# One scale for fifteen weight tiles and one for v, found in the prologue of a hybrid attention block

## The chip, the cores and the metric

The kernel runs on one core of one Trainium2 chip. A core has five engines that run their own instruction streams side by side: TensorE (PE, with weight loads shown as PEld), VectorE (DVE), ScalarE (ACT), GpSimd (POOL), and SyncE (SP), which here issues nearly all DMA transfers. The metric is the time of one execution in device microseconds (us). Three runs of the kernel before took 502.83, 505.03 and 505.9 us; the median is 505.03.

## The reference

One encoder layer on 1024 tokens of width 1024, in float32. One projection gives the queries, keys, values and gates of two head groups. Group A has 8 heads with a neighbourhood of 8 rows x 16 columns on a 16 x 64 token grid and a learned bias per head. Group B has 8 query heads on 2 key/value heads, rotary positions, a window of 128 tokens to each side and a sink logit.

```python
h = x @ w_in                                   # 1024 x 3328
q_a, k_a, v_a, z_a, q_b, k_b, v_b, z_b = split(h)   # 512 x4, 512, 128, 128, 512
y_a = neighborhood_attention(q_a, k_a, v_a, rel_pos_bias)
y_b = windowed_gqa_with_sink(rotary(q_b), rotary(k_b), v_b, sink)
mixed = concatenate([y_a * silu(z_a), y_b * silu(z_b)])
y = mixed @ w_out
out = layer_norm(2 ** 0.25 * x + y, ln_gain, ln_bias)
```

## The kernel before

**Numbers.** For accuracy near float32 a product is made of three passes over a high and a low part of each operand. For q, k and z the parts are float16: `x` is scaled by a power of two that suits its largest absolute value and split into `xf` (L477, L482). The weights of a *column tile* (128 of the columns of `w_in`, in two halves of 256 KB) are scaled by a power of two too. The power comes from the sum of the tile's absolute values: ScalarE sums each half with an Abs activation (`w_scan`, L183), one small matmul with a matrix of equal entries adds the 128 partitions (L196, "the total"), and a chain of some eight small VectorE instructions (L200 to L215) makes from it the scale `wsc`, its inverse `inv`, and what later steps need of it: `sg` for the scores, `rsg` for the bias, `vscb` for the gates. `w_split` then makes the float16 halves `wh` (ScalarE, L164) and `wl` (GpSimd, L169 and L170).

**The stages.** First the V projection in another format with three passes (L431, to 63.7 us); beside it `x` is loaded a second time and split. `v` has a scale per column group: VectorE keeps a running maximum `vmax` over all of v (L497, L498), five transposes bring it to where it can be reduced (`v_scale`, L566), five more spread the result (`v_spread`, L580), and `v_part` (L594) scales, casts and splits each of 8 row blocks and writes them to DRAM, from where `window` (L797) copies four windows for group A. At the same time the first 6 column tiles of 21 (NPRO = 6; `ORDER` gives zb0, z0, zb1, kb, qb0, z1) are projected. Each takes 48 matmuls of 128x512 (`project`, L332, the matmul is L356); the events of the V part are hung on the count of these 288 matmuls by `run_to`.

Then comes the attention in 128 units (64 of group B, then 64 of group A). A unit is: scores (L703, L704), a VectorE instruction that adds the bias and finds the maximum (L711), the exponential on ScalarE (L727), a split of the probabilities in two float16 parts (ScalarE L737, VectorE L738), a DMA transposition (L741), the products with v some units later (L766), and per four units the division by the sum (L775) and transposes (L786, "OT") in the bank "ot", whose result is multiplied by the gate. That bank is also the one into which the totals of L196 go. The remaining 15 column tiles and the first part of the output projection are fed between the units, about 6 matmuls per unit (`FILL_AT`, `pump_to`). The last stage is the output projection (L890) with the residual and the layer norm (`final`, L907).

**Order.** Within a `manual_schedule` region every engine gets its instructions as written. The kernel before has several such regions: the V part, the prologue tiles in two calls of `run_to`, and the attention with `final`; a planner may interleave instructions of different regions. What the column tiles need of ScalarE, VectorE, GpSimd and SP during the attention isn't written at its place but put in a queue per engine (`enq`). Per unit `pop` takes ND = 1 instruction (or a chain as one) from VectorE's queue, NA = 1 from ScalarE's and NP = 2 from GpSimd's, those with the lowest `prio` first; the chain of a scale has priority 0. `need` forces what must come before the next step. `rope` makes the rotary parts of q and k of group B (cast L286, shuffle L287, products L288 and L289, sum L290), and `split_q` and `split_k` the two parts of q and k (`hi` L234 and L236 on ScalarE, `lo` L240 and L242 on VectorE).

**Buffers.** `x` in its three-pass format fills 16 buffers of 4 KB per partition (`big`). The float16 `xf` takes 8 of them again when the V projection is through with them; the others stay empty until the output weights come. Weight halves go through four buffers `wr`: the load of half m + 4 (L153) is issued when `w_split` of half m is done.

Of the kernel before, what the change touches and what calls it, by code (L numbers as in the profile page):

```python
# [30 lines left out]
NPRO = 6  # L31
FILL = ORDER[NPRO:]
# [18 lines left out]
def hybrid_block(ctx, tc, xT, x, wt, wv, wo, bias, sink, gain, lbias, cos, sin, bmask, out):  # L51
# [4 lines left out]
    big = ctx.enter_context(tc.tile_pool(name="big", bufs=16))  # L56
# [13 lines left out]
    def pair_tile(name):  # L70
        return big.tile([128, 2, 512], F32R, tag="big", name=name)

    xh, xl, x16h, x16l = {}, {}, {}, {}
    for half in range(2):
        for k in range(KT):
            t = pair_tile(f"x{half}{k}")
            xh[half, k], xl[half, k] = t[:, 0, :], t[:, 1, :]
# [9 lines left out]
    vsc = const.tile([128, 6], F32, name="vsc")  # L87
    vscb = const.tile([128, 8], F32, name="vscb")
# [3 lines left out]
    wm = const.tile([128, 2 * NT], F32, name="wm")  # L92
    wg = const.tile([128, NT], F32, name="wg")
    wsc = const.tile([128, NT], F32, name="wsc")
    inv = const.tile([128, NT], F32, name="inv")
    sg = const.tile([128, 8], F32, name="sg")
    rsg = const.tile([128, 4], F32, name="rsg")
# [15 lines left out]
    ENG = ("act", "dve", "pool", "sp", "pe")  # L113
# [12 lines left out]
    def enq(eng, fn, *deps, prio=1):  # L126
        op = Op(eng, fn, deps, prio)
        if clock["step"] is None:
            op.emit()
        else:  # L130
            queues[eng].append(op)
        return op

# [22 lines left out]
    def w_split(m):  # L156
# [15 lines left out]
        scale = wsc[:, m // 2:m // 2 + 1]  # L172

        o = enq("act", hi, scale_ops[m // 2], prio=0.5)
# [4 lines left out]
    w_ops, stk_ops, load_ops, scale_ops, scan_ops = {}, {}, {}, {}, {}  # L179

    def w_scan(m):
        def scan():
            nc.scalar.activation(junk, raws[m].rearrange("p k c -> p (k c)"), AF.Abs, accum_out=wm[:, m:m + 1])  # L183

        if m < NH:
            scan_ops[m] = enq("act", scan, load_ops.get(("w", m)))

    def w_scale(n):
        if n >= NT:
            return  # L190
        name, cell = ORDER[n], {}
        kind, p = name.rstrip("0123"), int(name[-1]) if name[-1].isdigit() else 0

        def total():
            cell["ps"] = bank("ot")
            nc.tensor.matmul(cell["ps"][:, 0:2], ones, wm.bitcast(BF16)[:, 4 * n + 1:4 * n + 4:2], start=True, stop=True)  # L196

        def chain():
            g, ps, v = wg[:, n:n + 1], cell["ps"], inv[:, n:n + 1]
            nc.vector.tensor_reduce(g, ps[:, 0:2], axis=mybir.AxisListType.X, op=ALU.add)  # L200
            nc.vector.tensor_scalar_max(g, g, 2.0 ** -30)
            nc.vector.tensor_scalar(g.bitcast(I32), g.bitcast(I32), 0x7F800000, None, op0=ALU.bitwise_and)
            nc.vector.tensor_scalar(wsc[:, n:n + 1].bitcast(I32), g.bitcast(I32), 0x7F800000, None, op0=ALU.bitwise_xor)  # L203
            tanh = kind[0] == "z" and n > 2
            nc.vector.tensor_scalar(v, g, xrs, 0.25 if tanh else 0.5, op0=ALU.mult, op1=ALU.mult)
            if tanh:
                e, c = (4 + p, 4 + p // 2) if kind == "zb" else (p, p)
                nc.vector.tensor_mul(vscb[:, e:e + 1], vsc[:, c:c + 1], v)
            if kind[0] == "q":
                i = p if kind == "q" else 4 + p  # L210
                nk = ORDER.index("kb" if kind == "qb" else f"k{p}")
                nc.vector.tensor_scalar(sg[:, i:i + 1], v, inv[:, nk:nk + 1], -0.125 / QSCALE ** 2,
                                        op0=ALU.mult, op1=ALU.mult)
                if kind == "q":
                    nc.vector.reciprocal(rsg[:, p:p + 1], sg[:, p:p + 1])  # L215
# [167 lines left out]
    with ExitStack() as vctx:  # L383
# [119 lines left out]
        with tc.manual_schedule():  # L503
# [16 lines left out]
            for j in range(10):  # L520
                x2_load(j)
# [630 lines left out]
```

## Time and profile before

| | |
|---|---|
| median of 3 runs | 505.03 us |
| the profiled execution | 499.32 us, span 497.5 us |
| V projection | to 63.7 us |
| six prologue tiles | 63.7 to 138.3 us |
| attention and 15 tiles | 138.3 to 401.0 us |
| output projection | 401.0 to 489.5 us |
| last row's norm | 489.5 to 497.5 us |
| mean granted TensorE clock | 0.990 |

All durations below are of the profiled execution, which took 499.32 us by the same clock as the runs; its span is what the instructions cover. In the rows of groups stand the line, engine, operation, the tensors written and read, shapes and the count, then the busy time, the mean duration in ns, and the idle time of that engine just before, with what ended it. In the rows of waits stand the waiting instruction, what it waited for, and the total, the number of times and the longest in us. In timelines the first two numbers are start and length; matmuls overlap in the array, so a row of several can be longer than their distance.

### The profile page before, as it was taken

The page shows a single profiled execution, that of the slowest core. Times are in us where ns is not written, and L with a number is a line of the kernel's source. Part 1 is how long each engine was busy: PE and PEld are TensorE (multiplying, and loading weights), DVE is VectorE, ACT ScalarE, POOL GpSimd, SP SyncE. Part 2 cuts the span into 40 slices and gives each one's busy share as a digit, 9 for nine tenths or more (in the row PEclk, how much of TensorE's full clock was granted, in tenths as well). Part 3 has the DMA queues.
Part 4 walks back from the last instruction along what each step waited for, and adds up shares of the span by engine and source line. Part 5 has one row for each costly group of instructions (what it writes and reads, how often), then busy time and mean ns, then how long its engine had stood idle before and what let it go on. Part 6 is the DMA issues. An engine that isn't in the chain of part 4 may idle for free.

```text
span 497.5 us, 9558 instructions
## 1 busy us (share of the span) xinstructions
PE 457.3 (92%) x3262; PEld 296.1 (60%) x3262; DVE 371.6 (75%) x926; ACT 295.6 (59%) x701; POOL 225.5 (45%) x231
## 2 busy tenths in 40 slices
PE   8999999969899999798898898999999999999993
PEld 6999954423345455354455454556554677788883
DVE  5885979776657988887887877887777747559644
ACT  4639533544667887777778886877877737002101
POOL 0005943697437334854223745633674505314521
PEclk9999999998999999999899999999999999999998
DMA  7793141445546665576388999999986976535211
GB/s 254 260 293 129 60 143 43 127 127 170 190 90 142 108 136 109 114 121 116 90 170 205 204 208 197 235 215 207 224 176 157 208 166 232 174 145 190 107 42 63
DMA packets 134688, 78.95 MB, mean 159 GB/s; under 512 B 101360, under 2 KB 117744, under 8 KB 134384
## 3 DMA queue, kind: packets, MB, share of 16 engines
q1 hardware_dynamic: 134496, 78.20, 64.6%
q8 instruction: 25, 0.41, 0.4%
q14 instruction: 23, 0.19, 0.2%
q10 hardware_dynamic: 144, 0.15, 0.1%
HBM read 47.91 MB, written 9.96 MB: 116 GB/s over the span
## 4 chain that ended last, share of the span: by engine, by line
PE 31%; DVE 11%; ACT 4%; DMA 4%; issue 4%; SPq 1%; POOL 1%; ACTq 0%; DVEq 0%
PE ps_pj L356 12%; PE ps_s L890 4%; PE ps_pj L890 4%; PE ps_t L890 3%; PE ps_t L766 3%; DMA tr<-split 3%; DVE split L738 2%; DVE sn L711 2%; PE ps_ot L890 2%; PE ps_s L703 1%; PE ps_s L704 1%; DMA wor<-in_wo 1%; DVE m L824 1%; ACT split L737 1%; DVE qs L240 1%
## 5 line engine op out<-in xcount | busy, mean ns | idle before, releaser
L356 PE MATMUL ps_pj<-xf,wh 128*128 128x512 f16 x672 | 204.0, 382 | 5.5 <-DVE qs L240 3.3
L356 PE MATMUL ps_pj<-xf,wl 128*128 128x512 f16 x336 | 128.3, 382 | 0.0
L356 PEld LDWEIGHTS <-wh 128*128 128x128 f16 x672 | 62.6, 98 | 75.5 <-issue 9.2
L727 ACT ACTIVATE ps_s<-sn,nm 128x385 f32<-128x385 f32 (+3 forms) x128 | 70.4, 550 | 46.4 <-DVE nm L711 45.3
L738 DVE SCALAR_TENSOR_TENSOR split<-ps_s,split 128x384 f16<-128x384 f32 (+2 forms) x128 | 65.6, 512 | 28.1 <-ACT split L737 27.3
L169 POOL TENSOR_SCALAR wr<-wr,wsc 128x512 f32<-128x512 f32 x42 | 34.8, 827 | 98.4 <-ACT wh L164 93.9
L737 ACT ACTIVATE split<-ps_s 128x384 f16<-128x384 f32 (+2 forms) x128 | 57.4, 448 | 6.7 <-DMA tr<-split 4.9
L356 PEld LDWEIGHTS <-wl 128*128 128x128 f16 x336 | 33.0, 98 | 38.6 <-issue 1.1
L170 POOL TENSOR_TENSOR wl<-wr,wh 128x512 f16<-128x512 f32 x42 | 50.7, 1209 | 3.4
L703 PE MATMUL ps_s<-ks,qs 128*128 128x384 f16 (+2 forms) x128 | 39.8, 311 | 12.2 <-DVE split L738 7.6
L711 DVE CUSTOM_DVE_ANT_0 sn<-ps_s,bm,nsk 128x384 f32<-128x384 f32 (+1 forms) x64 | 40.8, 638 | 7.4 <-PE ps_s L704 6.8
L711 DVE CUSTOM_DVE_ANT_0 sn<-ps_s,bias,sg 128x288 f32<-128x288 f32 (+1 forms) x64 | 36.0, 563 | 12.7 <-PE ps_s L704 12.0
L704 PE MATMUL ps_s<-ks,qs 128*128 128x384 f16 (+2 forms) x128 | 39.7, 311 | 0.0
L766 PEld LDWEIGHTS <-tr 128*128 128x128 f16 (+1 forms) x1104 | 36.6, 98 | 2.0 <-issue 0.3
L164 ACT ACTIVATE wh<-wr,wsc 128x512 f16<-128x512 f32 x42 | 29.8, 711 | 12.4 <-DVE wsc L203 4.8
L678 POOL TENSOR_SCALAR bias<-bias,rsg 128x576 f32<-128x576 f32 (+1 forms) x24 | 19.2, 801 | 32.7 <-DMA bias<-in_bias 23.6
L945 ACT ACTIVATE sd<-mv,eps 128x1 f32<-128x1 f32 x8 | 2.4, 295 | 53.0 <-DVE mv L943 53.0
L890 PE MATMUL ps_s<-wo,m 128*128 128x512 f32 (+1 forms) x144 | 32.7, 375 | 0.3 <-DVE m L824 0.3
L270 POOL COPY ks<-ks 64x512 f16<-64x512 f16 x40 | 25.5, 644 | 9.9 <-ACT ks L234 3.7
L890 PE MATMUL ps_pj<-wo,m 128*128 128x512 f32 (+1 forms) x120 | 28.9, 378 | 0.7 <-DVE z L316 0.7
L890 PEld LDWEIGHTS ps_s<-wo,m 128*128 128x128 f32 x144 | 25.4, 188 | 5.6 <-DVE m L824 0.7
L704 PEld LDWEIGHTS <-qs 128*128 128x128 f16 x128 | 12.5, 98 | 26.6 <-issue 14.1
(154 smaller groups left out, 872.0 us busy)
## 6 DMA issues: line engine op xcount, KB each, us to landing
wr<-in_wt SPq DMA_DIRECT2D x42, 256.0 KB, 3.0
xraw<-in_xT SPq DMA_DIRECT2D x31, 256.0 KB, 3.5
bias<-in_bias SPq DMA_DIRECT2D x16, 288.0 KB, 3.4
wor<-in_wo SPq DMA_DIRECT2D x16, 256.0 KB, 5.7
xr<-in_x SPq DMA_DIRECT2D x8, 512.0 KB, 6.5
out<-xr SPq DMA_DIRECT2D x14, 256.0 KB, 2.0
bias<-in_bias SPq DMA_DIRECT2D x8, 384.0 KB, 3.9
wvraw<-in_wv SPq DMA_DIRECT2D x7, 320.0 KB, 4.5
```

The source lines that it names most:

```text
L164: nc.scalar.activation(h, raws[m], AF.Copy, scale=scale)
L169: nc.gpsimd.tensor_scalar(raw, raw, scale, 1.0, op0=ALU.mult, op1=ALU.mult)
L170: nc.gpsimd.tensor_sub(l, raw, h)
L356: nc.tensor.matmul(ps, a[:, k % 4, :], mv, start=(k == 0 and i == 0), stop=(k == KT - 1 and i == 2))
L703: nc.tensor.matmul(ps[:, :n], q, sl[0], start=True, stop=False)
L704: nc.tensor.matmul(ps[:, :n], q, sl[1], start=False, stop=True)
L711: nc.vector.tensor_tensor_reduce(sn[:, :n], ps[:, :n], bias_t, sg[:, c:c + 1], init, op0=ALU.add, op1=ALU.min, accum_out=nm)
L727: nc.scalar.activation(pt[:, :m], sn[:, :m], AF.Exp, bias=nm, scale=-1.0, accum_out=sm[:, k:k + 1])
L737: nc.scalar.activation(hl[:, :m, 0, :c], src, AF.Copy, scale=PSCALE)
L738: nc.vector.scalar_tensor_tensor(hl[:, :m, 1, :c], src, PSCALE, hl[:, :m, 0, :c], op0=ALU.mult, op1=ALU.subtract)
L766: nc.tensor.matmul(ps[:, HD * m:HD * m + HD], a, b_, start=(i == 0), stop=(i == len(mms) - 1))
L890: nc.tensor.matmul(ps, lh[:, ts], rh[:, cs], start=(e == EO[0] and i == 0), stop=(e == EO[-1] and i == 2))
```

## The change

The 15 column tiles of the attention get one common scale. In the prologue all 15 are loaded a first time, 512 KB each, into the buffers that `x` leaves free, 8 at a time (`sum_load`, at matmuls 1 to 8, and then each when a buffer is through). `sum_w` adds the absolute values of a whole tile in one instruction, at every 14th matmul from 28 on, on ScalarE (10 tiles) or VectorE (5). At matmul 237 `w_scale(NPRO)` makes one total of 15 columns and takes the largest, and one chain gives `wsc`, `inv`, `sg`, `rsg`, `vscb` and `invt` for all of them. With that, scans, totals and chains are no longer in the attention, TensorE's queue is dropped, and the tiles are still loaded by `w_load` for their split as before.

`v` gets one scale too. `v_max` reduces each row block of 640 columns in one VectorE instruction, `v_scale` (now at matmul 12, before at 66) needs one transposition and gives `vrs` and `vsc`. The multiplication of L605 is gone: the cast takes the scale. The copy `vb` goes from GpSimd to VectorE. `v_part` stands at matmuls 24 + 9t instead of 90 + 9t, and `window` at 124 + 12b instead of 178 + 14b.

The ordered region reaches from the V part to the end of the attention, and `final` stands behind it, outside. In the prologue the steps of `rope`, `split_q` and `split_k` are no longer emitted at once but at given numbers of matmuls later (`after`). ScalarE's queue counts as long from 5 waiting instructions instead of 3. The core of the diff:

```diff
-    big = ctx.enter_context(tc.tile_pool(name="big", bufs=16))
+    big = ctx.enter_context(tc.tile_pool(name="big", bufs=8))
+    def big_tile(name, shape=(128, 2, 512), dt=F32R):
+        n = taken[0]
+        taken[0] += 1
+        tag = "big" if n < 8 or 16 <= n < 24 or n >= 32 + NS else "big2"
+        return big.tile(list(shape), dt, tag=tag, name=name)
...
+    def enq(eng, fn, *deps, prio=1, after=0):
+        if clock["step"] is not None:
+            queues[eng].append(op)
+        elif after:
+            events.setdefault(ran[0] + after, []).append(op.emit)
+        else:
+            op.emit()
...
-        scale = wsc[:, m // 2:m // 2 + 1]
+        g = min(m // 2, NPRO)
+        scale = wsc[:, g:g + 1]
...
     def w_scale(n):
+        c, m = (2 * n, 2) if n < NPRO else (2 * NPRO, NS)
+        ps = bank("ot")
+        nc.tensor.matmul(ps[:, :m], ones, wm.bitcast(BF16)[:, 2 * c + 1:2 * (c + m):2], start=True, stop=True)
+        nc.vector.tensor_reduce(g, ps[:, :m], axis=mybir.AxisListType.X, op=ALU.add if n < NPRO else ALU.max)
...
+        if n == NPRO:
+            for i, (a, b) in enumerate(((nk, nq), (nk, NPRO), (NPRO, NPRO))):
+                nc.vector.tensor_scalar(sg[:, i:i + 1], inv[:, a:a + 1], inv[:, b:b + 1], -0.125 / QSCALE ** 2,
                                         op0=ALU.mult, op1=ALU.mult)
+            nc.vector.reciprocal(rsg, sg[:, 2:3])
-        o = enq("pe", total, scan_ops[2 * n], scan_ops[2 * n + 1])
-        scale_ops[n] = enq("dve", chain, o, prio=0)
...
-            o1 = enq("act", hi, dep, prio=prio)
-            ops.append(enq("dve", lo, o1, prio=prio))
+            o1 = enq("act", hi, dep, prio=prio, after=16 if dep else 0)
+            ops.append(enq("dve", lo, o1, prio=prio, after=20 if dep else 0))
...
+        def v_max(t):
+            nc.vector.tensor_reduce(vm[:, t:t + 1], v32[t], axis=AXX, op=ALU.max, apply_absolute_value=True)
...
         def v_scale():
+            nc.vector.tensor_reduce(vg, vm, axis=AXX, op=ALU.max)
+            ps = bank("s")
+            nc.tensor.transpose(ps[:, :128], vg.to_broadcast([128, 128]), identf)
+            nc.vector.tensor_reduce(vg, ps[:, :128], axis=AXX, op=ALU.max)
...
         def v_part(t):
-                nc.vector.tensor_sub(vt[:, :, 1, :], v3, vt[:, :, 0, :])
-                nc.gpsimd.tensor_scalar_mul(vb[:, t - 1], vt[:, 8:10], 1.0)
+                nc.vector.scalar_tensor_tensor(vt[:, :, 1, :], v3, vrs, vt[:, :, 0, :], op0=ALU.mult, op1=ALU.subtract)
+                nc.vector.tensor_copy(vb[:, t - 1], vt[:, 8:10])
...
-                nc.vector.tensor_mul(v32[t], v32[t], scr)
-                nc.scalar.copy(vt[:, :, 0, :], v3)
+                nc.scalar.activation(vt[:, :, 0, :], v3, AF.Copy, scale=vrs)
...
+        def sum_load(i):
+            if i < NS:
+                sums[i] = big_tile(f"ws{i}", (128, 2, 4, 128), F32)
+                nc.sync.dma_start(sums[i], wt[NPRO + i].rearrange("h p k c -> p h k c"))
+
+        def sum_w(i):
+            t, c = sums.pop(i).rearrange("p h k c -> p (h k c)"), 2 * NPRO + i
+            if i % 3 != 1:
+                nc.scalar.activation(t, t, AF.Abs, accum_out=wm[:, c:c + 1])
+            else:
+                nc.vector.tensor_reduce(wm[:, c:c + 1], t, axis=AXX, op=ALU.add, apply_absolute_value=True)
+            sum_load(i + 8)
+
+        at(12, v_scale)
+        for t in range(9):
+            at(24 + 9 * t, v_part, t)
+        for i in range(8):
+            at(1 + i, sum_load, i)
+        for i in range(NS):
+            at(28 + 14 * i, sum_w, i)
+        for b in range(4):
+            at(124 + 12 * b, window, b)
+        at(237, w_scale, NPRO)
...
-            pop("act", NA if i < M_AT[0] and len(queues["act"]) < 3 else 2)
+        pop("act", NA if i < M_AT[0] and len(queues["act"]) < 5 else 2)
...
+    ordered.close()
+    final()
```

406 lines of the change are left out of this document (175 added, 231 removed).

## The prediction

> **What bounds the kernel now.** I read the page's totals and its 40 slices first, then a table of busy time by stage, then the waits of TensorE in the longest stage, and last the order of single instructions around the largest waits.
>
> ```profile
> span 497.5 us, 9558 instructions
> PE 457.3 (92%) x3262; PEld 296.1 (60%) x3262; DVE 371.6 (75%) x926; ACT 295.6 (59%) x701; POOL 225.5 (45%) x231
> ...
> PEclk9999999998999999999899999999999999999998
> ```
>
> TensorE works 92% of the span, and no other engine over 75%. So the time is TensorE's work plus its gaps. The change adds no matmul of weight and takes only small ones away, so the question is which gaps go and which come. The table by stage (start:end, length, then busy time with instruction counts of PE, PEld, DVE, ACT, POOL, granted clock, DMA share, GB/s):
>
> ```profile
> 63.70:138.30 74.60, 65.39 (x304) 29.28 (x303) 55.53 (x117) 35.14 (x65) 42.90 (x42) 0.98 0.43 134
> 138.30:401.00 262.70, 242.21 (x2103) 135.34 (x2102) 207.78 (x619) 201.68 (x527) 130.01 (x143) 0.99 0.81 164
> 401.00:489.50 88.50, 87.54 (x468) 72.04 (x467) 55.14 (x102) 20.35 (x38) 29.94 (x22) 1.00 0.45 148
> 489.50:497.50 8.00, 0.00 (x0) 0.00 (x0) 4.18 (x9) 1.44 (x3) 1.68 (x2) 0.81 0.19 66
> ```
>
> The first row is the stage of the six prologue tiles, the second the attention with the other 15, the third the output projection with TensorE full, the fourth the last row's normalization. The attention has 262.70 - 242.21 = 20.5 us of idle TensorE. The waits there, TensorE's alone:
>
> ```profile
> PE ps_s L703 <- DVE split L738: 7.6, 9, 2.8
> PE ps_ot L786 <- DVE wg L200: 4.0, 4, 1.5
> PE ps_pj L356 <- DVE qs L240: 3.3, 3, 1.8
> PE ps_s L703 <- DVE sn L708: 2.2, 2, 1.9
> PE ps_pj L356 <- DVE ks L240: 2.2, 3, 1.0
> PE ps_pj L890 <- DVE z L316: 0.7, 1, 0.7
> ```
>
> They add to 20.0 us, nearly all of the idle time, and every one is for VectorE.
>
> **The attention, part by part.** Removed there are 26 scans on ScalarE, the 14 totals on TensorE, and 14 chains of small instructions on VectorE, one per later tile:
>
> ```profile
> L183 ACT ACTIVATE junk<-wr 128x512 bf16<-128x512 f32 x26 | 16.0, 616 | 0.0
> L183 ACT ACTIVATION_READ_ACCUMULATOR junk<-wr 128x1 f32 x26 | 4.9, 188 | 0.0
> L205 DVE TENSOR_SCALAR inv<-wg,xrs 128x1 f32<-128x1 f32 x14 | 2.8, 203 | 0.0
> ...
> L215 DVE RECIPROCAL rsg<-sg 128x1 f32<-128x1 f32 x4 | 0.7, 165 | 0.1
> ```
>
> ScalarE loses 16.0 + 4.9 = 20.9 us of its 201.7. The eight rows of VectorE's chain run from 2.8 us down to 0.7, some 14 us of its 207.8. Neither engine is full, so this work is worth nothing by itself. It counts where it stands ahead of something that TensorE waits for.
>
> (a) The OT transposes (L786) share their one bank with the totals, and wait for the chain to read it. Without totals this wait is gone: **4.0 us**. What is late next there is the divided output of L775, which the order has three units earlier, so I count nothing back.
>
> (b) The waits of L356 for the second parts of q and k (3.3 + 2.2) come from deferred instructions. VectorE takes one deferred instruction per unit (ND = 1), and the chain has priority 0. In the units where it takes the turn, the second `lo` of a q or k half slips one unit, and the next column tile's group finds its bank still in use. In the changed order that `lo` stands one unit earlier at those places (units 36, 60, 76, 84, 92 and 108 where before had the next one). Of 5.5 us I take **4.3**, since the casts ahead of the `lo` are now spread one per unit and can leave the short waits; the bounds are 2 and 5.5.
>
> (c) Two of the larger waits for other things, and what follows one of them (start, length, what, and in brackets the idle time before):
>
> ```profile
> 206.21 0.32 PE L703 MATMUL ps_s<-ks,qs 128*128 128x384 f16 x1 [1.95 <-DVE sn L708]
> ...
> 237.40 0.27 PE L703 MATMUL ps_s<-ks,qs 128*128 128x256 f16 x1 [2.81 <-DVE split L738]
> ...
> 238.61 1.04 PE L356 MATMUL ps_pj<-xf,wh 128*128 128x512 f16 x2
> 239.45 0.63 PE L356 MATMUL ps_pj<-xf,wl 128*128 128x512 f16 x1
> ```
>
> Both stand where a chain took VectorE's turn from the shuffle of the rotary part, so that the GpSimd products of it came late, ScalarE waited in order, and exp and split behind it came late too. In the changed order the shuffle stands at units 27 and 43 instead of 30 and 46. I take **2.0** for the first and **2.0** of 2.8 for the second, bounds 0 and 4.8. The other eight waits for L738, 4.8 us, are the length of exp, split and transposition of the unit itself; I leave them.
>
> (d) After the 2.81 us gap the matmuls start 0.42 us apart (238.61 to 239.45 for two), and the granted clock stays low for a while:
>
> ```profile
> 220.00:240.00 20.00, 17.19 (x169) 9.72 (x168) 13.80 (x42) 14.12 (x37) 10.58 (x11) 0.96 0.57 108
> 240.00:260.00 20.00, 18.86 (x150) 10.20 (x149) 17.60 (x50) 14.69 (x39) 5.61 (x6) 0.95 0.69 136
> ```
>
> That is 0.04 x 20 + 0.05 x 20 = **1.8 us**, back if the gap goes; else nothing. The Trainium skill speaks against taking it as the price of this gap: by "TensorE: Matmul & The Clock Gate", section "What's actually happening", the clock halves after a whole idle window of some 3.4 us, and 2.81 is less. By that rule this term would be nothing and the time 1.8 us higher. The trace has half speed right behind this gap, so I keep it.
>
> Attention: 4.0 + 4.3 + 2.0 + 2.0 + 1.8 = **14.1 us**.
>
> **The prologue, built anew.** Its six tiles are 288 matmuls. Where nothing interrupts them they take
>
> ```profile
> 340.26 1.29 PE ps_pj L356 x6
> ```
>
> 0.215 us each: 61.9 us at least, of the 74.6 measured. So 12.7 us are lost there before, the largest piece a total that waited 5.20 us for its scan behind the k casts, then ran at half speed:
>
> ```profile
> 112.87 0.16 PE L196 MATMUL ps_ot<-wm,ones 128*128 128x2 bf16 x1 [5.20 <-ACT junk L183]
> 112.90 1.01 PE L356 MATMUL ps_pj<-xf,wh 128*128 128x512 f16 x2
> ...
> 115.41 0.72 PE L356 MATMUL ps_pj<-xf,wh 128*128 128x512 f16 x2
> ```
>
> The six matmuls from 112.90 to 115.41 took 2.51 us instead of 1.29; with a few more, 1.4 us lost. In the changed order that scan stands at matmul 168 and the casts at 184, so this gap goes. The first attention unit's scores move from about matmul 238 to the end, so their wait for q goes too, as do the ten transposes of the v scale but one.
>
> What comes new is **v's single scale**. Its transposition stands on TensorE behind matmul 12, at 63.72 + 12 x 0.215 = 66.3. It waits for eight reductions on VectorE, and six of these stand behind the negation of the sink, which waits for a load:
>
> ```profile
> 64.43 0.43 SPq L537 DMA_DIRECT2D sk<-in_sink  x1
> ...
> 66.93 0.17 DVE L541 TENSOR_SCALAR nsk<-sk 128x8 f32<-128x8 f32 x1 [2.83 <-DMA sk<-in_sink]
> ...
> 36.37 0.17 DVE L530 TENSOR_REDUCE gm<-xm 128x1 f32<-128x16 f32 x1
> ...
> L440 DVE TENSOR_REDUCE xm<-x x16: 677/680/682, 20.2 to 35.7; 128x1 f32<-128x512 f32 x16
> ```
>
> A reduction of 512 elements took 0.68 us and one of 16 0.17, so one of 640 comes to about 0.81, my estimate. Six after 67.1 end at 72.0, and the small one of `vg` at 72.2: TensorE waits 72.2 - 66.3 = **5.8 us**, with all of tile 1 queued behind the transposition. By the gap at 112.87 another **1.4** goes at half speed (bounds for both: 4 and 8). One transposition takes 0.2.
>
> The sums of the 15 tiles lie beside the matmuls: ten Abs passes of 1024 on ScalarE (by L183's 0.616 + 0.188 for 512 about 1.2 us each) and five reductions on VectorE, one every 14 matmuls or 3.0 us. Between matmuls 24 and 96 ScalarE also has eight v casts,
>
> ```profile
> L606 ACT CAST vt<-v x8: 724/725/726, 86.0 to 105.5; 128x640 f16<-128x640 f32 x8
> ```
>
> and with scans, splits, outputs and three or four Abs passes I count 16.6 us of work in 15.5. I take **1.0** for that, bounds 0 and 3. The one total over 15 columns stands at matmul 237, 13 matmuls behind the last sum, 2.8 us for 1.2 us of work; I count nothing, and a wait there is in the 3.
>
> **The loads** are the unknown term. Fifteen of 512 KB, eight in one burst at about 68 us, pass through the one SP queue ahead of the weight loads that the prologue needs. Up to the load of half tile 9 I count 9.4 MB: 13 sums, three weight halves, cos and sin, six v parts. Its scan is needed at matmul 138: 63.7 + 5.8 + 1.4 + 138 x 0.215 = 100.6, less 0.8. So 9.4 MB have 31.6 us, or 0.297 MB/us. What the trace shows as rate:
>
> ```profile
> 280.00:300.00 20.00, 18.76 (x188) 11.11 (x189) 16.07 (x51) 15.40 (x43) 10.59 (x12) 1.00 1.04 207
> 20.00:40.00 20.00, 20.00 (x138) 20.00 (x138) 15.31 (x26) 10.01 (x23) 0.00 (x0) 1.00 0.83 263
> ...
> GB/s 0 0 0 0 0 0 0 0 0 0 0 0 246 322 291 299 174 56 229 393 328 361 415 382 377 388 328 131 33 0 0 0 0 0 0 0 0 0 0 0
> ```
>
> The first row is full engines with transpositions of many small packets among them (207); the second large rows at 0.83 of the engines' time, so 317 if full; the third the 15 us around 67, where cos, sin and weights alone were under way (40 slices of 0.375 us), with up to 415. A weight load took 3.0 us to land:
>
> ```profile
> wr<-in_wt SPq DMA_DIRECT2D x42, 256.0 KB, 3.0
> ```
>
> The sums have rows of 2 KB like the weights, but the v parts have short ones. At 0.263 everything is 4 us late, at 0.317 nothing. The nearest row is the second, at its full rate; I take **0.5**, bounds 0 and 4.4 (and 17, the rival below).
>
> Prologue after: 61.9 + 5.8 + 1.4 + 0.2 + 1.0 + 0.5 = 70.8, so **3.8 us** gained, with bounds of -3 and +8.
>
> **The end.** The final part is now outside the written order. The planner sets the gain's load earlier and three copies of output weights on VectorE ahead of the splits of m, and one matmul group stands ahead of the last OT transposes. The third stage has only 88.50 - 87.54 = 1.0 us idle, so there is nothing to win: I charge **1.4**, bounds 0 and 4.
>
> **Sum**: -14.1 - 3.8 + 1.4 = -16.5 us. The profiled execution took 499.32 us (497.5 of span and 1.8 around it), so its like would take 482.8. The median of the runs is 505.03, 5.7 above the profiled one; on that scale the time is **488.5**. The bounds of (b) to (d), of the prologue and of the end reach some 17 us to the slow side if all fall together and 14 to the fast one; a third of each is my range for this case alone, 483 to 494.
>
> **Rivals.** (1) *The loads decide; slower than before.* If the burst moves at the 207 GB/s of the full engines, the load of half tile 11 (12.4 MB behind 68.2) lands at 128.1 instead of the 110.9 at which its total stands: 17.2 us more of idle TensorE, and another 1.4 at half clock. Then 505.03 - 16.5 + 16.7 + 1.4 = 506.6. It decides when the rate falls under about 0.21 MB/us; above 0.3 it costs nothing. For it: one queue, and v's short packets in it. Against it: 263 at 0.83, and 415. The Trainium skill, "DMA: Bandwidth & Descriptors", section "Queues, rings and completion order", says that a queue's descriptors are taken in ring order on each DMA engine, so a weight load would not pass the sums; no row of before shows such a jam. (2) *The attention's waits are put off, not removed.* exp, split and transposition of a unit bound the rest, and what (b) to (d) give comes back as waits for L738. Then only 4.0 of 14.1 is kept: -4.0 - 3.8 + 1.4 = -6.4, 498.6. For it: L738 already leads the waits, and VectorE is 79% busy in that stage. Against it: most waits sit at the units where a chain stood. (3) *All waits go.* 20.0 + 1.8 in the attention, the prologue's +5.3 with neither load nor ScalarE waits, and no loss at the end: -27.1, 477.9.
>
> **Chances.** Forecast 0.57, (2) 0.20, (1) 0.13 with what lies between it and the forecast, (3) 0.07, and 0.03 for a time beyond all of these. One per cent, 5 us, is about what a measurement tells from no change. Faster by more than that (under 500): all of the forecast and (3), most of (2): 0.78. Slower (over 510): a third of (1) and the rest, 0.08; within 1% 0.14. The range goes from 480, half way from the forecast's low end to (3), to 504, into what lies between the forecast and (1); it leaves out most of (3) and of (1).
>
> **What the changed profile would show.** The waits of L786 for `wg` and most of those of L356 for L240 are absent; the attention stage is some 248 us; the clock rows are 0.99 or more. A gap of 5 to 6 us ends at the transposition of `vg` near 72, then matmuls start 0.42 us apart. No total (L196's successor) waits long for a scan; if one does, and the load before it took far more than 3 us to land, rival 1 is at work. The last stage stays within 2 us of 88.5. I am wrong if L738's waits grow past 12 us, if the prologue takes over 76 us, or if the last stage takes over 92.

## The result and the profile after

The changed kernel's median is 483.02 us (480.12 to 483.77, four runs), that of the kernel before 503.93 us with its fourth run (500.16 to 505.9). The ratio is 0.958, 95% interval 0.951 to 0.966: faster. Run again beside other kernels it gave 481.09 us and 0.959 (0.956 to 0.963). The prediction was 488.5 in a range of 480 to 504.

The page of the changed kernel: span and busy time of the engines, and the clock in 40 slices.

```profile
span 482.0 us, 9415 instructions
PE 452.4 (94%) x3239; PEld 294.5 (61%) x3239; DVE 349.4 (73%) x820; ACT 286.9 (60%) x661; POOL 216.1 (45%) x223
...
PEclk9999978999999999999998999999999999999997
```

Its time by stage, cut where the first prologue matmul, the 289th, the second unit's scores, the last unit's scores and the last matmul lie (columns as in the prediction):

```profile
61.56:135.85 74.29, 65.41 (x298) 29.20 (x297) 47.37 (x97) 42.96 (x78) 34.68 (x37) 0.93 0.72 243
137.14:385.28 248.14, 237.94 (x2076) 134.75 (x2075) 200.09 (x538) 185.78 (x477) 129.72 (x142) 0.99 0.93 174
385.28:474.00 88.72, 87.55 (x470) 72.39 (x469) 55.34 (x102) 20.07 (x38) 31.33 (x22) 1.00 0.43 141
474.00:482.00 8.00, 0.00 (x0) 0.00 (x0) 4.05 (x9) 1.44 (x3) 1.68 (x2) 0.63 0.18 66
```

Cut at the same instructions, the kernel before had 63.72 us to the first prologue matmul, 75.73 from there to the 289th, 261.60 of attention and 96.78 to the end:

| stage | before | after | difference | predicted |
|---|---|---|---|---|
| V projection | 63.72 | 61.56 | -2.2 | 0 |
| six tiles (1st to 289th matmul) | 75.73 | 74.29 | -1.4 | -3.8 |
| attention (2nd to last unit's scores) | 261.60 | 248.14 | -13.5 | -14.1 |
| from there to the end | 96.78 | 96.72 | -0.1 | +1.4 |
| span | 497.5 | 482.0 | -15.5 | -16.5 |

(The second unit's scores started 0.3 us before the 289th matmul in the one and 1.3 behind it in the other, which makes +1.6 in the sum. In the changed kernel six matmuls of the seventh tile stand ahead of these scores, in the kernel before none; so 1.3 of the attention's 13.5 us are work that only changed sides, and 12.2 are gained.) So the attention gave most of the gain. In the prologue one gap was exchanged for another.

The medians are 20.9 us apart, 5 more than the profiled executions. The profiled execution of the kernel before was the shortest of its first four at a granted clock of 0.990; its 36 runs beside the experiments (six slow ones left out) had 0.974 to 0.992, those of the changed kernel 0.98 to 0.99. Of the 36, the ten with a clock of 0.987 or more took 499.7 us on average, the nine under 0.980 took 504.1. So I read the rest of the difference as clock that the kernel before loses in most of its runs; the two go together in the runs, but no experiment changed the clock alone.

The waits of TensorE in the attention of the changed kernel (in us: total, times, longest):

```profile
PE ps_s L696 <- DVE split L731: 3.4, 8, 1.0
PE ps_s L696 <- DVE sn L701: 2.7, 2, 2.3
PE ps_t L759 <- DMA tr<-split: 2.3, 4, 1.6
PE ps_pj L881 <- DVE z L312: 0.7, 1, 0.7
PE ps_pj L348 <- POOL wl L183: 0.6, 1, 0.6
```

They were 20.0 us and are 9.7. Those of the OT transposes and of the q and k parts (4.0 and 5.5) are gone, those for the split (now L731) fell from 7.6 to 3.4, and 2.3 us of waits for the DMA transposition are new.

The timeline of TensorE and then that of VectorE in the changed kernel's prologue, at v's scale:

```profile
71.76 0.48 PE L550 MATMUL ps_s<-identf,vg 128*128 128x128 f32 x1 [7.44 <-DVE vg L548]
72.03 1.06 PE L348 MATMUL ps_pj<-xf,wh 128*128 128x512 f16 x2
72.88 0.63 PE L348 MATMUL ps_pj<-xf,wl 128*128 128x512 f16 x1
```

```profile
66.98 0.17 DVE L525 TENSOR_SCALAR nsk<-sk 128x8 f32<-128x8 f32 x1 [8.70 <-DMA sk<-in_sink]
67.06 4.45 DVE L483 TENSOR_REDUCE vm<-v 128x1 f32<-128x640 f32 x6
71.54 0.16 DVE L548 TENSOR_REDUCE vg<-vm 128x1 f32<-128x8 f32 x1
```

TensorE stood for 7.44 us behind a transposition that waited for six reductions, and these waited for the load of the sink, 4 KB that v's scale has no use for. Behind it two matmuls took 0.85 us, half speed. A second wait of the prologue is new too and stands in no term of the prediction: the 289th matmul waits for the gate `z`.

```profile
135.85 0.59 PE L348 MATMUL ps_pj<-xf,wh 128*128 128x512 f16 x2 [1.44 <-DVE z L312]
```

### The profile page after: what moved, and what is told of

The parts are those of the page before. It is cut to its first block, busy times and chain, and to the rows that moved or that the text cites. A ratio compares the mean times of both kernels' runs of the same rounds, so it can differ in the third digit from the quotient of the medians.

```text
span 482.0 us, 9415 instructions
## 1 busy us (share of the span) xinstructions
PE 452.4 (94%) x3239; PEld 294.5 (61%) x3239; DVE 349.4 (73%) x820; ACT 286.9 (60%) x661; POOL 216.1 (45%) x223
## 3 DMA queue, kind: packets, MB, share of 16 engines
q1 hardware_dynamic: 138576, 86.07, 74.3%
## 4 chain that ended last, share of the span: by engine, by line
PE 46%; DVE 16%; DMA 14%; ACT 8%; issue 8%; POOL 4%; SPq 3%; POOLq 0%; ACTq 0%; DVEq 0%
PE ps_pj L348 21%; PE ps_pj L881 5%; PE ps_s L881 5%; PE ps_t L759 4%; PE ps_t L881 3%; DMA tr<-split 3%; DMA wr<-in_wt 3%; PE ps_s L696 3%; PE ps_s L697 3%; DVE qs L237 3%; DMA xraw<-in_xT 2%; DVE split L731 2%; PE ps_ot L881 2%; DMA wvraw<-in_wv 2%; DVE sn L704 1%
## 5 line engine op out<-in xcount | busy, mean ns | idle before, releaser
L348 PEld LDWEIGHTS <-wh 128*128 128x128 f16 x672 | 64.2, 99 | 64.9 <-issue 4.3
L731 DVE SCALAR_TENSOR_TENSOR split<-ps_s,split 128x384 f16<-128x384 f32 (+2 forms) x128 | 65.6, 513 | 29.2 <-ACT split L730 28.2
L182 POOL TENSOR_SCALAR wr<-wr,wsc 128x512 f32<-128x512 f32 x42 | 30.6, 729 | 85.1 <-ACT wh L177 69.3
L265 POOL COPY ks<-ks 64x512 f16<-64x512 f16 x40 | 26.8, 675 | 10.8 <-ACT ks L229 7.0
L973 POOL TENSOR_TENSOR xr<-xr,gb 128x512 f32<-128x512 f32 x7 | 10.3, 1483 | 40.4 <-ACT xr L970 40.4
```

The source lines that it names most:

```text
L182: nc.gpsimd.tensor_scalar(raw, raw, scale, 1.0, op0=ALU.mult, op1=ALU.mult)
L348: nc.tensor.matmul(ps, a[:, k % 4, :], mv, start=(k == 0 and i == 0), stop=(k == KT - 1 and i == 2))
L731: nc.vector.scalar_tensor_tensor(hl[:, :m, 1, :c], src, PSCALE, hl[:, :m, 0, :c], op0=ALU.mult, op1=ALU.subtract)
```

## The experiments

The names of the kernels are those of their results. Unless said otherwise, "attention" is the stretch from the second unit's scores to the last unit's, and "prologue" that from the first prologue matmul to the 289th, both of the profiled execution. In the changed kernel they take 248.1 and 74.3, when run again 247.7 and 72.7. Some expectations name 136.5 and 75 us for the 289th matmul of the changed kernel, 64.7 for that of sink_late_nosums and 71.0 for that of sums_spread. These count two or three matmuls too far; the values are 135.85, 74.3, 64.05 and 70.55.

### The changed kernel again (after_again)

> The changed kernel once more, as the base for the kernels beside it. Every theory: 480 to 485, a ratio to the kernel before of 0.95 to 0.966, the wait for vg between 5 and 7.5 us.

481.09 us, ratio 0.959 (0.956 to 0.963). The wait for `vg` was 5.22 us in place of 7.44, since the sink landed 2.1 us earlier; the prologue is shorter by 1.6, as the half speed behind the gap lasted longer (13 steps of 0.427 us for 11). The gap thus varies by 2 us between executions.

### Scans alone, back in the attention (scans_back)

```diff
+    def scan_back(m):
+        if m < NH and clock["step"] is not None:
+            enq("act", lambda: nc.scalar.activation(junk, raws[m]..., AF.Abs, accum_out=wm2[:, m:m + 1]),
+                load_ops.get(("w", m)))
```

> Edit: in the changed kernel the 26 Abs scans of half tiles stand again in ScalarE's queue during the attention, their results unused; no totals, no chains. Theory A (what counted were the totals in the OT bank and the chains' turns on VectorE): the attention, from the second unit's scores to the last unit's, is 248 to 251 us as against 248.1 in the changed kernel and 261.6 before. Theory B (ScalarE's 20.9 us counted): 255 us or more.

477.81 us, ratio 0.946 (0.943 to 0.949). Its attention, by the same window:

```profile
135.25:380.04 244.79, 235.99 (x2076) 134.17 (x2075) 199.40 (x536) 199.47 (x529) 129.89 (x142) 1.00 0.91 177
```

ScalarE is busy 13.7 us longer than in the changed kernel (199.47 against 185.78), and the attention isn't longer: it is 3 us shorter, with no drop of the clock in it. The scans' work on ScalarE was worth nothing. That they make it shorter I don't claim; the ratio's interval lies apart from the changed kernel's in the other group of runs, and no run tells why.

### Totals and chains, back in the attention (chains_back)

```diff
+        for m in (2 * n, 2 * n + 1):          # scans of one element each
+            if m not in scan_ops:
+                scan_back(m)
+        o = enq("pe", total, scan_ops[2 * n], scan_ops[2 * n + 1])
+        scale_ops[n] = enq("dve", chain, o, prio=0)
-        o = enq("act", hi, load_ops.get(("w", m)), prio=0.5)
+        o = enq("act", hi, load_ops.get(("w", m)), scale_ops.get(m // 2), prio=0.5)
```

> Edit: in the changed kernel 13 totals into the OT bank and 13 chains of six small VectorE instructions with priority stand again in the attention, each behind two scans of one element on ScalarE; the results are unused. Theory A (totals and chains counted): the waits of the OT transposes come back with about 4 us, those of the q and k second parts with 3 to 5, the attention takes 255 to 262 us. Theory B (the scans' time counted): 248 to 251 us. If only the 4 us of the OT transposes come back, the attention takes about 252.

500.84 us, ratio 0.991 (0.988 to 0.994): the gain is gone but for one per cent. The attention and TensorE's waits in it:

```profile
134.64:399.34 264.70, 239.54 (x2089) 133.78 (x2088) 208.32 (x614) 190.00 (x529) 128.66 (x142) 0.99 0.82 164
```

```profile
PE ps_s L731 <- DVE split L766: 6.3, 7, 1.7
PE ps_s L731 <- DVE sn L736: 4.2, 3, 1.9
PE ps_pj L383 <- POOL wl L186: 3.6, 3, 1.5
PE ps_ot L814 <- DVE ch L219: 2.9, 4, 0.9
PE ps_pj L383 <- ACT wh L180: 2.6, 2, 2.0
PE ps_pj L383 <- ACT ks L264: 1.8, 1, 1.8
PE ps_pj L383 <- DVE qs L270: 1.7, 2, 0.9
PE ps_pj L383 <- DVE ks L270: 0.9, 1, 0.9
```

13 small matmuls, 26 reads of one element and 13 chains cost 16.6 us of attention (264.7 - 248.1), a little past the 255 to 262 expected. 2.9 us of it is the OT bank (the 4.0 of before) and 1.7 + 0.9 the q and k parts. The waits for the weights' parts `wl` and `wh` (3.6 + 2.6) weren't there before, though there too a tile was split only behind its chain; why they appear here isn't shown. So 16.6 us is what totals and chains cost in this order, and not the 12.2 that were gained.

### The kernel before without totals (no_total)

```diff
-            nc.vector.tensor_reduce(g, ps[:, 0:2], axis=mybir.AxisListType.X, op=ALU.add)
+            src = cell["ps"][:, 0:2] if "ps" in cell else wm[:, 2 * n:2 * n + 2]
+            nc.vector.tensor_reduce(g, src, axis=mybir.AxisListType.X, op=ALU.add)
...
+            scale_ops[n] = enq("dve", chain, scan_ops[2 * n], scan_ops[2 * n + 1], prio=0)
```

> Edit: the kernel before without the totals on TensorE during the attention: each chain reads the scans' sums of its own partition instead of the sum over all 128 partitions, so that step of the scale is left out. Scans and chains stay, and a chain still takes VectorE's one turn; chains and the rotary shuffles come some units earlier, since they no longer wait for a total's place. Theory A (the total's place and its bank make the price): the attention takes 247 to 253 us instead of 261.6. Theory B (scans' and chains' work on their engines make it): 258 or more.

493.79 us, ratio 0.979 (0.971 to 0.987).

```profile
139.15:392.74 253.59, 239.94 (x2084) 134.17 (x2082) 209.01 (x618) 199.95 (x527) 129.99 (x142) 1.00 0.84 169
```

The attention is 253.6 us, 8.0 less than before and 0.6 past the upper end of theory A. The total and its place in the order make some two thirds of the attention's 12.2 us (the kernel before and no_total both have the six matmuls in this stage). It is more than the 4.0 us of its bank: without the wait for a total's place the rotary shuffles stand at units 27 and 43 as in the changed kernel, the 2.81 us gap is 0.66, and the clock is 1.00 throughout.

### The chain's turn on VectorE (chain_own_turn, no_total_own_turn)

```diff
+            need(*[o for o in scale_ops.values() if o.step is None
+                   and all(d.step is not None and d.step + d.lag < i for d in o.deps)])
             pop("dve", ND if i < M_AT[1] else 2)
```

> Edit: the kernel before, with one difference: the chain of a scale no longer takes VectorE's one turn per unit, another deferred instruction goes as well. Scans, totals in the OT bank and the chains' work stay. Theory A (half of the gain is the turn, half the bank): the waits for the second parts of q and k and the 2.81 us gap go, those of the OT transposes stay, the attention takes 250 to 254 us instead of 261.6. Theory B (the chain's own time or the bank is what costs): 258 or more.

> Edit: as without the totals, and the chain doesn't take VectorE's turn. Theory A: what the turn costs shows only here, 1 to 3 us less attention than without the totals alone, close to the changed kernel's 248.1. Theory B: as without the totals alone, within 1 us, or slower.

With totals 504.07 us, ratio 1.004 (0.999 to 1.008); without them 494.03, 0.982 (0.976 to 0.989). The attentions, the first kernel's and then the second's:

```profile
143.62:407.41 263.79, 243.42 (x2096) 135.81 (x2095) 207.79 (x618) 200.95 (x527) 129.10 (x142) 0.99 0.81 162
```

```profile
143.39:398.93 255.54, 240.31 (x2084) 134.04 (x2082) 210.16 (x618) 199.71 (x527) 129.51 (x142) 1.00 0.85 167
```

Both are some 2 us longer than the same kernel with the turn taken (261.6 and 253.6): theory B in both. In the first, some 1.7 of the 2.2 us come from a second stretch of half clock (212.2 to 215.5, granted clock 0.50). Its waits for the q and k parts did fall, from 5.5 to 2.3 us, but those for the split rose from 7.6 to 8.9 and those for L708 from 2.2 to 3.2. The turn alone was not the price: the rows read as if the instruction that went earlier took VectorE's time from the unit's own steps instead. The gap at the 49th unit stayed (2.92 us). In the chain of waits of that kernel it goes back through the gate's tanh on ScalarE to a rotary product on GpSimd:

```profile
240.00 1.23 POOL rp_raw L288
...
241.26 0.03 ACT z L315
...
242.56 0.39 ACT split L737
...
242.97 0.04 DVE split L738
```

The gate tile zb3 has the buffer of the cosines (`ZTAG`), so its tanh waits for their last reader, and the split of a unit waits behind it in ScalarE's order.

What is left between no_total (253.6) and the kernels without chains (244.8 and 248.1) is 5 to 9 us, 4 to 7.5 without the six matmuls, and they differ in the chains on VectorE, in ScalarE's scans (but for scans_back), in the prologue and in the threshold of ScalarE's queue. That the chains' own 14 us make it is the likeliest, but no run has them alone.

### The sink's negation behind v's scale (sink_late)

```diff
-                nc.vector.tensor_scalar_mul(nsk, sk, -1.0)
...
         at(12, v_scale)
+        at(20, nc.vector.tensor_scalar_mul, nsk, sk, -1.0)
```

> Edit: the negation of the sink on VectorE moves from the V part to matmul 20, behind v's scale. The changed kernel waited 7.44 us for vg at 71.76 and then ran 37 matmuls at a slower pace, some 2.3 us lost. Theory A (the wait is nothing but the sink's load ahead of the reductions): the reductions end near 63, the wait is under 1 us, no half clock behind it, the 289th matmul starts 8 to 10 us earlier than 136.5 (126.5 to 128.5), the time falls to 473 to 476. Theory B (the prologue is held by its loads, and the wait only covered them): waits for ws or wr loads, or for ScalarE behind them, take its place, the 289th matmul starts after 131, the time is 479 or more.

479.55 us, ratio 0.950 (0.947 to 0.954). The gap of 7.44 us is gone altogether, but the prologue takes 70.48 us, 2.2 to 3.8 less than in the two profiles of the changed kernel instead of 8 to 10, and the 289th matmul starts at 132.38: theory B. Two new gaps on TensorE, and two waits of ScalarE ahead of them:

```profile
76.92 0.39 PE L348 MATMUL ps_pj<-xf,wl 128*128 128x512 f16 x1 [1.32 <-POOL wl L183]
...
86.04 0.16 PE L202 MATMUL ps_ot<-wm,ones 128*128 128x2 bf16 x1 [2.91 <-ACT junk L196]
```

```profile
72.28 1.06 ACT L587 ACTIVATE ws<-ws 128x1024 f32<-128x1024 f32 x1 [2.86 <-DMA ws<-in_wt]
...
85.27 0.63 ACT L196 ACTIVATE junk<-wr 128x512 bf16<-128x512 f32 x1 [1.58 <-DMA wr<-in_wt]
```

The first sum waits for its load and holds ScalarE, which works in order; later a scan waits for a weight half. The DMA traffic of this kernel from 62 to 100 us (40 slices of 0.95 us, then loads with count, size and median us to landing):

```profile
GB/s 0 190 299 193 336 405 282 229 282 354 401 403 410 407 412 405 410 403 410 413 351 374 381 400 379 391 375 356 386 384 332 314 243 336 362 392 402 399 351 289
...
ws<-in_wt SPq DMA_DIRECT2D x15, 512.0 KB, 8.2
...
wr<-in_wt SPq DMA_DIRECT2D x7, 256.0 KB, 5.8
```

The engines are full at some 400 GB/s, and a weight half takes 5.8 us to land there, where the median of the kernel before was 3.0. So the wait for `vg` had been covering the burst, and rival 1's mechanism exists: at 400 GB/s it costs a few us, at the 207 of the prediction's bound it would have cost 17.

### Without loads and sums (sink_late_nosums)

```diff
-        for i in range(8):
-            at(1 + i, sum_load, i)
-        for i in range(NS):
-            at(28 + 14 * i, sum_w, i)
+    nc.vector.memset(wm, 32.0)
```

> Edit: as in the kernel with the late sink, and the 15 loads of 512 KB and the 15 sums are left out; the shared scale comes from a constant instead, so the output is only right as far as that constant suits. Theory A (the loads and sums are hidden): within 1.5 us of the kernel with the late sink, at the 289th matmul and in all. Theory B (the loads hold up the weight loads, or the sums hold up ScalarE): the 289th matmul starts more than 2 us earlier than there.

474.72 us, ratio 0.941 (0.937 to 0.945). The prologue takes 64.05 us, 6.4 less than with loads and sums, against 61.9 of bare matmuls. So with the gap out of the way the loads and sums together cost 6.4 us, more than the 1.5 that were counted (1.0 and 0.5); theory B. This run leaves out both, so it doesn't tell one from the other.

### The loads spread, the sums earlier (sums_spread, sums_early)

```diff
-        for i in range(8):
-            at(1 + i, sum_load, i)
         for i in range(NS):
-            at(28 + 14 * i, sum_w, i)
+            at(4 + 11 * i, sum_load, i)       # sums_spread: 6 + 13 i
+            at(38 + 12 * i, sum_w, i)         # sums_spread: 45 + 13 i
...
-            sum_load(i + 8)
```

> Edit: as in the kernel with the late sink, but the 15 loads are issued one by one at matmuls 6 + 13 i, each 39 matmuls ahead of its sum at 45 + 13 i, instead of eight in a burst. With the late sink alone the 289th matmul started 70.5 us after the first, without loads and sums 64.7; its burst held weight loads back (5.8 us to land) and ScalarE waited for both. Theory A (the order of the loads is the cost): 65 to 66.5 us to the 289th matmul, 475 to 477 in all. Theory B (the bytes or the work of the sums are the cost): 69 us or more, 479 or more.

> Edit: as in the kernel with spread loads, but load i at matmul 4 + 11 i and sum i at 38 + 12 i, the last at 206 instead of 227. With spread loads the first 193 matmuls had no wait left, and 1.7 and 3.1 us came at matmuls 216 and 235, where ScalarE stood before the rotary part. Theory A (the last sums stood too close to the total): 65 to 67 us from the first to the 289th matmul instead of 71.0, 473 to 477 us in all. Theory B (the rotary part itself holds up ScalarE): a wait of 2 us or more stays between matmuls 200 and 240, 478 or more.

sums_spread: 480.52 us, ratio 0.958 (0.953 to 0.963), prologue 70.55, theory B's figure. Up to the 193rd matmul it lost almost nothing (41.7 us against 41.3 at 0.215 each), then came, on TensorE,

```profile
111.12 0.59 PE L348 MATMUL ps_pj<-xf,wh 128*128 128x512 f16 x2 [1.66 <-ACT rp_raw L281]
118.88 0.18 PE L202 MATMUL ps_ot<-wm,ones 128*128 128x15 bf16 x1 [3.06 <-ACT wh L177]
```

and on ScalarE ahead of them

```profile
109.44 1.06 ACT L587 ACTIVATE ws<-ws 128x1024 f32<-128x1024 f32 x1 [5.56 <-DMA ws<-in_wt]
```

a sum that waited 5.56 us for its load, which had been issued on the same queue between the copies of v's windows. That points to where a load stands in the queue, and not to the bytes or the sum's work; no run moved that load alone.

sums_early: 475.12 us, ratio 0.945 (0.938 to 0.952). The prologue takes 67.80 us and the attention 245.37. One gap of 2.12 us for `wl` stays at the 255th matmul. That lies between the theories, nearer to A. By its median it is the fastest kernel of the study that leaves nothing out, 6 us under the changed kernel's 481.09; the two weren't run in one group, but their ratios' intervals (0.938 to 0.952, 0.956 to 0.963) don't meet.

### The last query parts one by one (sums_early_q)

```diff
+        for d in (2, 1):
+            if i + d in (16, 32):
+                need(stk_ops[f"b{(i + d) // 16}"][4 - d])
```

> Edit: as with the early sums, and the last second parts of the rotary queries, which a new head pair takes all at once before its first scores (two of 64x512 at unit 32), are taken one each in the two units before (60 and 62 of the rows instead of 64 twice; at unit 16 alike). In the changed kernel the scores at 200.62 waited 2.35 us, and at 193.31 with the early sums 2.15, as at 206.21 before (1.95), which the prediction put down to a chain. Theory A (the two forced instructions, 2.4 us on VectorE in a row, are that wait): it falls under 0.8 us, the attention is 1 to 2 us shorter than with the early sums (245.4), the time 473 to 475.5. Theory B (something else holds VectorE there): a wait of 1.5 us or more stays at that unit.

476.76 us, ratio 0.950 (0.945 to 0.954): no gain. First sums_early, then this kernel, TensorE around the 33rd unit:

```profile
193.31 0.32 PE L694 MATMUL ps_s<-ks,qs 128*128 128x384 f16 x1 [2.15 <-DVE sn L699]
```

```profile
188.93 0.27 PE L694 MATMUL ps_s<-ks,qs 128*128 128x256 f16 x1 [1.55 <-DVE split L729]
192.56 0.32 PE L694 MATMUL ps_s<-ks,qs 128*128 128x384 f16 x1 [0.99 <-DVE split L729]
```

The wait for the two forced instructions is gone, and 2.5 us of waits for the split stand in its place; the attention is 247.3 instead of 245.4. Theory A named the wait rightly and its worth wrongly.

## Why the prediction was right, step by step

**The attention** came out at 13.5 us for 14.1, or 12.2 without the work that changed sides, but by a different sum.
- (a) The wait of the OT transposes for `wg`, 4.0, went as predicted.
- (b) The waits for the q and k parts went altogether, 5.5 for the 4.3 taken. The cause given, the chain's turn, doesn't carry that: with the turn given back, these waits fell to 2.3 and the attention got no shorter. The step that failed is "in the units where it takes the turn, the second `lo` slips one unit", as a price: the slip is real, and its repair alone is worth nothing.
- (c) The first of the two waits stayed: 1.95 before, 2.35 after, by the same unit. In the changed kernel it reads

```profile
200.62 0.32 PE L696 MATMUL ps_s<-ks,qs 128*128 128x384 f16 x1 [2.35 <-DVE sn L701]
```

and on VectorE ahead of it stands

```profile
197.06 2.41 DVE L237 TENSOR_TENSOR qs<-rp_raw,qs 64x512 f16<-64x512 f32 x2 [0.32 <-ACT qs L231]
```

two query parts that a new head pair forces at once. No chain was in it; the last experiment confirms the two. The second wait, 2.81 us, went whole, for 2.0 taken, and by the way given: the shuffle earlier, so that the gate's tanh finds the cosines read. But "a chain took VectorE's turn from the shuffle" doesn't carry this. Before, the scores of 48 units had started when this shuffle ran. With the turn given back it was 46, and the gap stayed (2.92 us); in no_total, where a chain still takes the turn, it was 44 as in the changed kernel, and the gap was 0.66. What had held the shuffle was the wait for a total's place.
- (d) The clock came back at that place (1.00 from 212 to 252), but in this execution another came at 260 to 300, behind one of the new waits for a transposition:

```profile
260.77 0.51 PE L759 MATMUL ps_t<-vb,tr 128*128 128x64 f16 x9 [1.64 <-DMA tr<-split]
```

```profile
260.00:300.00 40.00, 39.23 (x321) 21.71 (x322) 30.93 (x83) 29.40 (x77) 25.44 (x33) 0.96 1.12 225
```

0.04 x 40 = 1.6 us against 1.8 before: nothing gained in this execution. When the changed kernel was run again the attention had no drop (1.00), so the term held there. The page of the Trainium skill that was weighed against this term, "TensorE: Matmul & The Clock Gate", section "What's actually happening", would have had no fall behind a gap of 2.81 us. The runs side with the trace: half speed also followed the gaps of 2.92 us in chain_own_turn and of 2.91 in sink_late.
- Left at zero, the other waits for the split fell from 4.8 to 3.4, and 2.3 us of waits for the transposition came in. These are the terms that were not in the sum.

**The prologue** gained 1.4 us for 3.8, and the V projection 2.2, which was counted as unchanged. That the whole of the profiled executions (15.5 us for 16.5) came so near is luck in this part: the V projection and the end made up for the prologue. The new gap was placed rightly, with its cause: 5.8 us predicted, 7.44 and 5.22 measured. In the larger one `vg` was there at 71.7, as predicted for 72.2, but TensorE came 2 us earlier, at 64.3; in the other the sink landed earlier too. The half speed behind it cost some 2.3 us (eleven steps of 0.427 us in place of 0.216) for 1.4. The 1.44 us of the 289th matmul came in besides. The old 5.20 us gap went as predicted, but the offsets in the prologue account for only a part of it. With them taken out,

```diff
-        elif after:
+        elif after and not NOW:
```

> Edit: in the changed kernel the steps of the rotary part and of the q and k parts in the prologue are emitted at once again, as before the change. Theory A (the 5.20 us gap of before was the scan standing behind the k casts): a gap of 3 to 6 us with a slow stretch behind it comes back near the 185th matmul, the 289th matmul starts 79 to 82 us after the first instead of 75, the time is 4 to 7 us above the changed kernel's. Theory B (that gap went because VectorE lost the multiplications and maxima of v): no such gap, within 2 us of the changed kernel.

the kernel (no_offsets) took 490.80 us, ratio 0.978 (0.974 to 0.982), 9.7 us above the changed kernel in the same group where 4 to 7 were expected, with two gaps on TensorE besides that for `vg`:

```profile
113.79 0.16 PE L203 MATMUL ps_ot<-wm,ones 128*128 128x2 bf16 x1 [1.65 <-ACT junk L197]
129.94 0.17 PE L203 MATMUL ps_ot<-wm,ones 128*128 128x15 bf16 x1 [4.95 <-ACT ws L589]
```

Near the 185th matmul 1.65 of the 5.20 us came back, less than the 3 to 6 expected; what took the rest away isn't shown (theory B's lighter VectorE is open). The larger loss is at the new total of 15 columns, where the last sum stands behind casts that wait for the rotary part. So the offsets guard a place that the kernel before didn't have, and the parts of the change can't be priced one by one and added.

**The loads and sums** were sized rightly only because the other gap covered them: 1.5 us taken, next to nothing in the changed kernel (its prologue has no wait but those for `vg` and `z`), 6.4 without the cover. Rival 1 fell with its rate: the burst moved at 400 GB/s, near the 415 of the 15 us row, not at the 263 or 317 that the prediction leaned on.

**The end**: 1.4 charged, 0.1 gained. The planner's other order of the loads and copies cost nothing; TensorE's stretch to its last matmul is 88.72 us after and 88.78 (489.50 - 400.72) before.

**Rival 2**, waits that are put off and not removed, wasn't what the change did, but it is what the single repairs in the attention did (the own turn, the query parts). The change escaped it since it took work and a place in the order away.

**The median** lies 5.5 us under the forecast. The sum was made on the profiled execution and moved by its distance to the median, 5.7, as if the changed kernel had the same distance. It has none: its profiled execution took 483.77 with a median of 483.02. That step was the largest miss.

## What to carry to other kernels

Work that is small on every engine can still cost through the place that it holds in an order: thirteen totals and chains of a microsecond, put back, cost 16.6 us of attention, while 13.7 us more of ScalarE's time cost nothing. Moving an instruction to close one gap moved the gap when the engine behind it stayed as busy; taking the instruction away closed it. Before a gap is repaired, ask what it covers: a wait of 5 to 7 us here hid a burst of loads, and taking it away shortened the stage by 2.2 to 3.8.

## What the runs showed of the hardware that was not expected

Up to the last matmul the granted clock fell to 0.50 for 3.41 us each time, or two or three times as long, and it fell a whole number of 3.41 us after it had first risen to 1.00. Cut into such windows, the 14 profiles have 1890 at full clock. After each of the 20 windows in which TensorE was idle for 2.03 us or more the clock fell, after none of the 1866 with 1.82 us or less, and after two of the four between (1.84 to 1.95). So in these traces a gap counts by how much idle time, with its neighbours, lies in one window. The changed kernel has both cases. The wait of 2.35 us that ended at 200.62 lay across two windows, and the clock stayed. The one of 1.64 us that ended at 260.77 lay in a window with 3.40 - 1.56 = 1.84 us of idle time, and the clock fell:

```profile
257.60:261.00 3.40, 1.56 (x35) 1.22 (x34) 2.04 (x6) 2.24 (x7) 0.61 (x1) 1.00 1.05 245
261.00:264.40 3.40, 3.40 (x17) 1.40 (x13) 1.59 (x4) 1.59 (x5) 0.63 (x1) 0.50 1.14 160
264.40:267.80 3.40, 3.40 (x18) 1.65 (x17) 2.13 (x9) 1.88 (x6) 3.10 (x5) 1.00 1.10 242
```

The first matmuls of the V projection run at half speed, 0.27 us apart instead of 0.15, for a time that varies. The granted clock rose to 1.00 at 9.8 us in the profile of the kernel before, at 9.9 in no_total, 7.2 in no_total_own_turn and 10.8 in chain_own_turn, but at 4.1 to 5.8 in the changed kernel (5.0) and all made from it. Half speed for 4.8 us more is 2.4 us, which fits the V projection's 2.2. Whether the change did it isn't settled: the four with the old V part have one instruction more on VectorE ahead of the first split (a fill of `vmax`, 0.59 us, over 1.5 us before the split starts), and nothing in the traces links it to the clock.

Loads with rows of 2 KB among them reached 401 to 413 GB/s for 9.5 us on end (sink_late, ten slices; 71 to 80 us has a DMA share of 1.05), where the attention with its transpositions shows 207 and 225 at as full engines (1.04 and 1.12). The rate to count with differed by a factor of two with what else was under way.
